# Two levels of seven products: where the inner seven stand among the outer ones, when their weights are split, and where one of their operands is kept

## The chip, the cores and the metric

The kernel runs on one core of a Trainium2 chip. The time is that of one execution on the device, in microseconds (us), and of several executions the median is taken. The engines of the core that matter here are TensorE (PE in the profile, with its weight loads shown apart as PEld), VectorE (DVE), ScalarE (ACT) and SyncE (SP), which issues nearly all transfers. Each engine works through its own list of instructions in a fixed order and waits at the head of that list until what the next instruction needs is there.

## The reference, cut to what matters

The program is a network of two layers over 1024 tokens of width 1024. Layer 0 mixes by attention, layer 1 by a gated recurrence, and behind each mixer stands the MLP that the change touches:

```python
def sqrelu_mlp(h, w_up, w_down):
    return jnp.square(jax.nn.relu(h @ w_up)) @ w_down

# in each of the two layers:
        h = rmsnorm(x, mlp_norm[layer])
        x = x + sqrelu_mlp(h, mlp_w_up[layer], mlp_w_down[layer]).astype(x.dtype)
```

Here `h` is 1024 by 1024 and `w_up` 1024 by 4096. The change is wholly in the product `h @ w_up`, called the up stage below; it comes once in each layer.

## The kernel before, in words

**A product in three.** All large products are made from float32 values that are split into a high part and a low part of the type that TensorE takes (`fp32r`). A split (`split`, `weight_split`, lines 458 and 469) is one copy that rounds, on ACT or DVE, and one subtraction on DVE. `mm3` (line 433) then issues three matmuls: high by high, high by low, low by high. A matmul has a 128x128 block of weights, and 512 columns of the other operand as a rule.

**The first level.** Each up stage works on 16 pairs of row blocks of the weights, `pair(m)` for m from 0 to 15 (line 757). A pair makes a 2 by 2 block of products by a Strassen scheme with seven products in place of eight. They are named 1 to 7 and stand in the order 1, 2, 5, 6, 3, 7, 4 (1, 5, 6, 2, 7, 3, 4 in the last pair). Each is 4 blocks times three matmuls of 512 columns, so twelve matmuls. Products 1, 6, 7 and 4 add up in one bank of PSUM (`main`), 5 and 3 in another (`side`), 2 in a third (`own`); between them the sums so far are copied out (`read`, `add_bank`). Behind the products stand the square of relu, the sums for the next Strassen scheme, and the stores of the results to DRAM (`kept`).

**The second level.** `INNER = (4,)` and `AT = 2` (lines 46 and 47): for the pairs from m = 4 on, product 4 of two neighbouring pairs, m and m + 1 with m even, is itself made by a Strassen scheme, in `inner` (line 693). So there are six groups of inner products in each layer, twelve in the kernel. Inner product k is two blocks times three matmuls of 256 columns, so six matmuls, and a group has 7 x 6 = 42. The inner products 1, 6, 7 and 4 add up in `main`, half of the first bank of the group; 5 and 3 in `side`, half of the second bank, and 2 in `own`, the other half of that second bank. After inner product 1, `take` (a copy on ACT or DVE) empties `main` before inner product 6 writes it, and so on. The order is fixed in lines 741 to 754: 1, take, 2, add, 6, take, 5, 7, take, add, 3, add, 4, take.

The weights of a group are four tiles: `a0`, `sa`, `sb`, and the far half of `a1`. They are split all together in lines 705 to 709, at the group's beginning. The other operands of inner products 5, 6, 7 and 4 are differences of quarters of `x[4]`; `prepare` (line 648) makes them once in each layer, during pair 2, splits them and stores the parts in DRAM, two transfers each. Each group loads them again, two tiles for each of these four inner products (lines 718 to 721). Inner products 1, 2 and 3 read halves of `x[4]` itself.

**What sets the order.** The code does not issue instructions as it runs. It first gives a list of operations to a planner (`Schedule`, line 146), which then places them on the engines by its own costs and latencies, always the ready operation of the lowest rank. The rank of a matmul is its place in the list (`now[i]`, line 205), counted in TensorE time; that of another operation is the time at which it is due. `lead = LEAD` brings it forward by 100 x 120 ns = 12 us. So what comes earlier in the list goes first on TensorE, as long as the planner believes it to be ready; otherwise TensorE gets the next one that is. The planner's beliefs that matter here: a matmul of 512 columns 216 ns; a slot of a ring of tiles usable 200 ns after its last reader; a copy of 512 columns 336 ns on DVE and 521 ns on ACT; a subtraction 603 ns; from DVE to TensorE 250 ns, from DVE to DVE 127 ns, from ACT to DVE 141 ns. Once placed, the order of each engine is fixed, and on the chip each engine waits for what is really there.

**Rings.** Tiles come from rings that are handed out in the order of the list: five slots for the high parts of weights (`wh`) and five for the low parts (`wl`), five for raw weights (`wr`), seven for sums of weights (`m`), twenty for other temporaries (`t`), four PSUM banks `p` (the banks of the inner groups and `own`) and four `q` (`main` and `side` of the pairs).

**Where the inner products stand.** In `pair`, the call `late = done[4]()` stands in the place of product 4 (lines 769 to 772). In the pair with even m this runs the whole of `inner`, so its seven products stand behind the six of the pair, one after another; the pair with m + 1 only takes the second half of the result.

Of the kernel before, what the change touches and what calls it, by code (L numbers as in the profile page):

```python
# [320 lines left out]
class Net:  # L321
# [326 lines left out]
    def prepare(self, name):  # L648

        near, far = slice(0, TH // 2), slice(TH // 2, TH)  # L650
        u = [self.t() for _ in range(HK)]
        for z, kept in zip(u, self.quarters[name]):
            self.dma(z, kept, 4 * P * TH)
        yield
        made = self.quarters[name] = {}

        def difference(out, x, y):
            for i in range(2):
                self.tt("any", out[:, i].only(i), x(i), y(i), ALU.subtract, TH // 2)

        def stored(k, t):
            made[k] = [self.keep(z.bitcast(F32)) for z in self.split(t.rearrange("p i c -> p (i c)"), self.t)]

        low, high = (lambda c: lambda i: u[i][:, c]), (lambda c: lambda i: u[2 + i][:, c])
        new = lambda: self.t(F32, (P, 2, TH // 2))
        part = lambda t: lambda i: t[:, i].only(i)
        t1 = new()
        difference(t1, low(far), low(near))
        stored(5, t1)
        yield  # L670
        t2 = new()
        difference(t2, high(far), part(t1))
        stored(6, t2)
        yield
        t3 = new()
        difference(t3, high(far), low(far))
        stored(7, t3)
        yield
        difference(t1, high(near), part(t2))
        stored(4, t1)  # L680
        yield

    def inner_of(self, name, m, x):
        got = []

        def of(i):
            if not got:
                got.extend(self.inner(name, m, x))
            return got[i]

        return of

    def inner(self, name, m, x):

        near, far, half = slice(0, TH // 2), slice(TH // 2, TH), TH // 2
        row, made = {2: 0, 4: 1}[name], self.quarters[name]
        self.s.lead = LEAD
        a0, a1 = (self.raw(self.io["up"][self.layer, i + row * (MT // 2)][:, TH:]) for i in (m, m + 1))
        sa, sb = self.t(tag="m"), self.t(tag="m")
        s1, s2, s3, s4 = sa[:, near].only(0), sa[:, far].only(1), sb[:, near].only(0), sb[:, far].only(1)  # L700
        self.tt("any", s1, a1[:, near], a1[:, far], ALU.add, half)
        self.tt("any", s2, s1, a0[:, near], ALU.subtract, half)
        self.tt("any", s3, a0[:, near], a1[:, near], ALU.subtract, half)
        self.tt("any", s4, a0[:, far], s2, ALU.subtract, half)
        wide = [self.weight_split(z) for z in (a0, sa, sb)]
        hi, lo = (self.tile(tag, BUFS[tag], (P, TH), F32R) for tag in ("wh", "wl"))
        self.copy(hi[:, far], a1[:, far], half, ("ACT", "DVE"), False)
        self.tt("any", lo[:, far], a1[:, far], hi[:, far].bitcast(F32), ALU.subtract, half)
        wide.append((hi, lo))
        w = {1: (0, near), 2: (0, far), 5: (1, near), 6: (1, far), 7: (2, near), 3: (2, far), 4: (3, far)}  # L710
        self.s.lead = 0
        banks = [self.psum(), self.psum()]
        main, side, own = banks[0][:, near].only(0), banks[1][:, near].only(0), banks[1][:, far].only(1)

        def product(k, ps, start):
            more = {} if start else {"skip_group_check": True}
            n, cols = w[k]
            if k in made:
                right = [self.t(F32R) for _ in range(2)]
                for z, kept in zip(right, made[k]):  # L720
                    self.dma(z.bitcast(F32), kept, 4 * P * TH)
            for i in range(2):
                c = slice(cols.start + i * P, cols.start + i * P + P)
                wh, wl = (z[:, c] for z in wide[n])
                if k in made:
                    xh, xl = (z[:, i * half : (i + 1) * half] for z in right)
                else:
                    at = near if k in (1, 2) else far
                    xh, xl = (z[:, at] for z in x[name][i if k == 1 else 2 + i])
                self.mm3(ps, (wh, wl), (xh, xl), start and i == 0, i == 1, half, slice(0, half), **more)  # L730

        y = [self.t(), self.t()]
        part = {(i, j): y[i][:, (near, far)[j]].only(j) for i in range(2) for j in range(2)}

        def take(z, bank):
            self.copy(halves(z), straight(bank), half)

        def add(z, bank):
            self.tt("DVE", halves(z), straight(bank), halves(z), ALU.add, half)

        product(1, main, True)
        take(part[0, 0], main)
        product(2, own, True)
        add(part[0, 0], own)
        product(6, main, False)
        take(part[0, 1], main)
        product(5, side, True)
        product(7, main, False)
        take(part[1, 1], main)
        add(part[1, 1], side)  # L750
        product(3, side, False)
        add(part[0, 1], side)
        product(4, main, False)
        take(part[1, 0], main)
        return y

    def pair(self, m, x, done, between=()):

        w = self.strassen_weights(*(self.io["up"][self.layer, i] for i in (m, m + MT // 2)), done)

        def read(ps):
            z = self.t()
            self.take(z, ps)
            return z

        main, side, own = self.psum("q"), self.psum("q"), None if 2 in done else self.psum()
        got = {}
        for name in (1, 5, 6, 2, 7, 3, 4) if m == MT // 2 - 1 else (1, 2, 5, 6, 3, 7, 4):
            if name in done:
                if name == 4:  # L770
                    late = done[4]()
                continue
            ps = main if name in (1, 6, 7, 4) else own if name == 2 else side
            self.product(ps, w[name], x[name], name in (1, 2, 5))
            if name == 1 and 2 in done:
                self.add_bank(done[2], main)
            elif name in (1, 5, 6, 7):
                got[name] = read(ps)
            for steps in between:
                next(steps, None)  # L780
        p5, u2, u3 = (got[name] for name in (5, 6, 7))

        def kept(name, z):
            self.hid[name, m] = self.keep(z)

        u1 = done[2] if 2 in done else got[1]
        if 2 not in done:
            self.add_bank(u1, own)
        h00 = self.square_relu(u1)
        kept(1, h00)  # L790
        self.add_bank(u2, side)
        h01, t5, t6, t4 = self.square_relu(u2), *(self.t() for _ in range(3))
        self.tt("any", t5, h01, h00, ALU.subtract)
        kept(5, t5)
        self.tt("any", p5, p5, u3, ALU.add)
        h11 = self.square_relu(p5)
        kept(3, h11)
        self.tt("any", t6, h11, t5, ALU.subtract)
        kept(6, t6)
        self.tt("any", h01, h11, h01, ALU.subtract)  # L800
        kept(7, h01)
        if 4 in done:
            self.tt("any", late, late, u3, ALU.add)
            h10 = self.square_relu(late)
        else:
            h10 = self.square_relu(main, True)
        kept(2, h10)
        self.tt("any", t4, h10, t6, ALU.subtract)
        kept(4, t4)

    def mlp(self, cut):

        x = self.mlp_second()
        steps = [self.prepare(name) for name in INNER]
        for m in range(0, MT // 2, 2):
            done = {}
            if m > AT:
                done = {name: self.inner_of(name, m, x) for name in INNER}
            for i in range(2):
                if m + i == MT // 2 - 2:  # L820
                    self.r = [self.a() for _ in range(NH)]
                    for hf in range(NH):
                        self.copy(self.r[hf], self.spread(self.square[hf]))
                if m + i == 1 and self.layer == 0:
                    self.hgrn_constants()
                self.pair(m + i, x, {name: y(i) if name == 2 else lambda y=y: y(i) for name, y in done.items()}, steps if m + i == AT else ())
        yield from self.down(cut)

    def hidden(self, name, p):
# [879 lines left out]
```

## Time and profile before

| what | value |
|---|---|
| median of 3 runs | 2011.96 us (2011.82 to 2012.09) |
| the profiled execution's own time | 2009.42 us |
| its span, first to last instruction | 2007.2 us |
| granted TensorE clock | 0.998 of full speed |
| VectorE busy | 1747.5 us (87%) |
| ScalarE busy | 1051.4 us (52%) |
| moved by DMA | 385.80 MB, 192 GB/s on average |

The up stage of layer 0 lies between about 325 and 605 us of the span, that of layer 1 between about 1420 and 1698 us. All instructions carry line 374, the line of the planner at which they are issued, so they are told apart by the tiles that they write and read: `q<-a,wh` with 512 columns are the outer products, `p<-a,wh` and `p<-t,wh` with 256 columns the inner products, where the operand read from `a` is `x[4]` and the one read from `t` has been loaded again from DRAM. `p<-a,wh` with 512 columns is product 2 of the pairs.

### The profile page before, as it was taken

The numbers are of one execution on the slowest core, as the hardware profiler recorded it, in microseconds if no ns is written. First come the engines' busy times: TensorE is split into PE (matmuls) and PEld (weight loads), VectorE is DVE, ScalarE is ACT, GpSimd is POOL, SyncE is SP. The second block draws the span as 40 slices with busy tenths as digits, with TensorE's granted clock in tenths as the row PEclk, the third lists the DMA queues.
The fourth block names the chain that finished last, engine by engine and source line by source line (L and its number), as shares of the span: only waits on it lengthen the run. The fifth ranks groups of instructions, "written<-read, shape, count | busy, mean of one in ns | idle before, by whom it ended". The sixth has DMA issues, their size and how long they took to land. (4 is left out here: it accounts for less than half of the span.)

```text
span 2007.2 us, 33753 instructions
## 1 busy us (share of the span) xinstructions
PE 1977.3 (99%) x11620; PEld 1720.8 (86%) x11620; DVE 1747.5 (87%) x3500; ACT 1051.4 (52%) x2141; POOL 62.2 (3%) x124
## 2 busy tenths in 40 slices
PE   9999999999999999999999999999999999999998
PEld 7877788888888888888888888888888888888887
DVE  8999899887788988799898999989987787897787
ACT  6567796555554423255345555554755556342353
POOL 4030100000000000000000000000000000000001
PEclk9999999999999999999999999999999999999999
DMA  6212364767678977745412212667577777897752
GB/s 217 89 53 63 122 225 156 275 216 231 231 228 287 312 262 259 237 163 175 146 62 80 76 59 90 206 205 255 179 248 231 231 226 246 290 324 230 234 180 84
DMA packets 218571, 385.80 MB, mean 192 GB/s; under 512 B 23968, under 2 KB 34208, under 8 KB 218400
## 3 DMA queue, kind: packets, MB, share of 16 engines
q1 hardware_dynamic: 217824, 383.13, 58.3%
q8 instruction: 91, 1.49, 0.3%
q14 instruction: 80, 0.66, 0.1%
q10 hardware_dynamic: 576, 0.52, 0.1%
HBM read 283.95 MB, written 99.61 MB: 191 GB/s over the span
## 5 line engine op out<-in xcount | busy, mean ns | idle before, releaser
L374 PE MATMUL q<-a,wh 128*128 128x512 f32 x2368 | 705.2, 379 | 1.8 <-DVE t L374 1.8
L374 PE MATMUL p<-a,wh 128*128 128x512 f32 (+1 forms) x2256 | 670.1, 376 | 0.8 <-DMA a<-d 0.6
L374 PEld LDWEIGHTS q<-a,wh 128*128 128x128 f32 x2368 | 445.6, 189 | 64.7 <-DVE t L374 2.6
L374 PEld LDWEIGHTS p<-a,wh 128*128 128x128 f32 x2256 | 417.3, 189 | 55.9 <-issue 1.2
L374 PE MATMUL q<-a,wl 128*128 128x512 f32 x1184 | 448.5, 379 | 0.0
L374 PE MATMUL p<-a,wl 128*128 128x512 f32 (+1 forms) x1128 | 421.4, 374 | 0.0
L374 ACT CAST a<-t 128x512 fp32r<-128x512 f32 x285 | 173.1, 619 | 272.6 <-PE q L374 138.9
L374 DVE TENSOR_TENSOR t<-t,t 128x512 f32<-128x512 f32 (+3 forms) x408 | 248.7, 633 | 22.2 <-ACT t L374 19.8
L374 ACT ACTIVATE t<-t 128x512 f32<-128x512 f32 x296 | 184.7, 630 | 140.4 <-DVE t L374 124.2
L374 PEld LDWEIGHTS q<-a,wl 128*128 128x128 f32 x1184 | 223.8, 189 | 31.3
L374 DVE TENSOR_TENSOR wl<-wr,wh 128x512 fp32r<-128x512 f32 x352 | 237.2, 676 | 11.6 <-ACT wh L374 4.1
L374 PEld LDWEIGHTS p<-a,wl 128*128 128x128 f32 x1128 | 213.6, 189 | 26.8 <-issue 0.4
L374 DVE TENSOR_TENSOR a<-t,a 128x512 fp32r<-128x512 f32 (+1 forms) x326 | 216.0, 682 | 4.5 <-ACT a L374 4.2
L374 DVE TENSOR_TENSOR wl<-m,wh 128x512 fp32r<-128x512 f32 x272 | 184.0, 684 | 7.5 <-ACT wh L374 1.9
L374 ACT CAST wh<-wr 128x512 fp32r<-128x512 f32 (+1 forms) x203 | 123.1, 609 | 121.8 <-PE p L374 45.2
L374 ACT COPY t<-q 128x512 f32<-128x512 f32 (+2 forms) x214 | 119.4, 560 | 88.4 <-PE q L374 86.9
L374 DVE TENSOR_TENSOR m<-wr,wr 128x512 f32<-128x512 f32 (+1 forms) x172 | 114.8, 669 | 39.5 <-DMA wr<-in_up 23.8
L374 ACT CAST wh<-m 128x512 fp32r<-128x512 f32 x166 | 101.4, 617 | 74.5 <-PE p L374 34.6
L374 PE MATMUL p<-wh,a 128*128 128x512 f32 x352 | 111.0, 385 | 0.0
L374 PEld LDWEIGHTS q<-t,t 128*64 128x64 f32 (+1 forms) x2160 | 95.1, 144 | 13.8 <-issue 6.2
L374 PE MATMUL q<-t,t 128*64 128x32 f32 (+2 forms) x2160 | 104.2, 229 | 1.6 <-DVE t L374 1.3
L374 DVE CAST wh<-wr 128x512 fp32r<-128x512 f32 x149 | 63.0, 423 | 46.1 <-PE q L374 22.1
(136 smaller groups left out, 2208.2 us busy)
## 6 DMA issues: line engine op xcount, KB each, us to landing
t<-d SPq DMA_DIRECT2D x368, 256.0 KB, 4.6
d<-t SPq DMA_DIRECT2D x300, 256.0 KB, 3.0
wr<-in_down SPq DMA_DIRECT2D x256, 256.0 KB, 4.1
wr<-in_up SPq DMA_DIRECT2D x152, 256.0 KB, 3.3
a<-d SPq DMA_DIRECT2D x60, 256.0 KB, 5.1
wr<-in_wqkv SPq DMA_DIRECT2D x48, 256.0 KB, 2.9
d<-a SPq DMA_DIRECT2D x48, 256.0 KB, 3.5
wr<-in_win SPq DMA_DIRECT2D x48, 256.0 KB, 2.9
```

The costliest lines, as they stand in the source:

```text
L374: fn(*[place(a) for a in args], **{k: place(v) for k, v in kw.items()})
```

## The change

The matmuls stay as they are, in number and size. What moves or is made another way:

1. `inner` becomes a generator that stops behind each of its products, and `pair` gets it in the list `between`: after each of its own products the even pair advances it by one. The list given to the planner then reads P1, I1, P2, I2, P5, I6, P6, I5, P3, I7, P7, I3, I4, where P are the products of the pair and I those of the group.
2. The weights of the group are split where the product stands that first uses them: `a0` ahead of I1, `sa` ahead of I6, `sb` ahead of I7, the far half of `a1` ahead of I4.
3. These splits, and the loads of the other operands, carry `lead = LEAD`; the loads did not before.
4. The operand of I5 is no longer split by `prepare` and stored in two parts, but stored once unsplit (so `prepare` also needs a fourth tile of its own, `t4`). A new generator, `put_in`, runs during pair 3: behind that pair's product 4 it loads the tile once and splits it into the far halves of `x[4][0]` and `x[4][1]`, which no inner product reads. I5 then reads it from there in each group, and the two loads for each group go away.
5. The result tiles `y` come into being inside the generator; `late = done[4]()` now only fetches them, and stands where the sum `late + u3` is made.

```diff
@@ prepare
         t1 = new()
         difference(t1, low(far), low(near))
-        stored(5, t1)
+        made[5] = self.keep(t1.rearrange("p i c -> p (i c)"))
         yield
...
-        difference(t1, high(near), part(t2))
-        stored(4, t1)
+        t4 = new()
+        difference(t4, high(near), part(t2))
+        stored(4, t4)
         yield
+
+    def put_in(self, name, x):
+
+        far, t1 = slice(TH // 2, TH), self.t()
+        for _ in range(6 if name == 4 else 1):
+            yield
+        self.dma(t1, self.quarters[name].pop(5), 4 * P * TH)
+        for i in range(2):
+            hi, lo, t = x[i][0][:, far].only(1), x[i][1][:, far].only(1), t1[:, i * (TH // 2) : (i + 1) * (TH // 2)]
+            self.copy(hi, t, TH // 2, ("ACT", "DVE"), False)
+            self.tt("any", lo, t, hi.bitcast(F32), ALU.subtract, TH // 2)
+        yield
@@ inner
-        wide = [self.weight_split(z) for z in (a0, sa, sb)]
-        hi, lo = (self.tile(tag, BUFS[tag], (P, TH), F32R) for tag in ("wh", "wl"))
-        self.copy(hi[:, far], a1[:, far], half, ("ACT", "DVE"), False)
-        self.tt("any", lo[:, far], a1[:, far], hi[:, far].bitcast(F32), ALU.subtract, half)
-        wide.append((hi, lo))
+        wide = []
         w = {1: (0, near), 2: (0, far), 5: (1, near), 6: (1, far), 7: (2, near), 3: (2, far), 4: (3, far)}
...
             n, cols = w[k]
+            self.s.lead = LEAD
+            if n == 3:
+                hi, lo = (self.tile(tag, BUFS[tag], (P, TH), F32R) for tag in ("wh", "wl"))
+                self.copy(hi[:, far], a1[:, far], half, ("ACT", "DVE"), False)
+                self.tt("any", lo[:, far], a1[:, far], hi[:, far].bitcast(F32), ALU.subtract, half)
+                wide.append((hi, lo))
+            elif n == len(wide):
+                wide.append(self.weight_split((a0, sa, sb)[n]))
             if k in made:
                 right = [self.t(F32R) for _ in range(2)]
                 for z, kept in zip(right, made[k]):
                     self.dma(z.bitcast(F32), kept, 4 * P * TH)
+            self.s.lead = 0
...
-                    xh, xl = (z[:, at] for z in x[name][i if k == 1 else 2 + i])
+                    xh, xl = (z[:, at] for z in x[name][i if k in (1, 5) else 2 + i])
...
-        y = [self.t(), self.t()]
+        y.extend(self.t() for _ in range(2))
...
         product(1, main, True)
         take(part[0, 0], main)
+        yield
         product(2, own, True)
         add(part[0, 0], own)
+        yield
         product(6, main, False)
         take(part[0, 1], main)
+        yield
         product(5, side, True)
+        yield
         product(7, main, False)
         take(part[1, 1], main)
         add(part[1, 1], side)
+        yield
         product(3, side, False)
         add(part[0, 1], side)
+        yield
         product(4, main, False)
         take(part[1, 0], main)
-        return y
+        yield
@@ pair
             if name in done:
-                if name == 4:
-                    late = done[4]()
                 continue
...
             for steps in between:
                 next(steps, None)
+        for steps in between:
+            run(steps)
...
         if 4 in done:
+            late = done[4]()
             self.tt("any", late, late, u3, ALU.add)
@@ mlp
+        made, n = {}, MT // 2
+        for m in range(n):
+            between, first = [], m - m % 2
+            if m == AT:
+                between += [self.prepare(name) for name in INNER]
+            if m == AT + 1:
+                between += [self.put_in(name, x[name]) for name in INNER]
+            for name in INNER:
+                c = first if name == 4 else first + 2
+                if AT < c < n and m % 2 == (name == 2):
+                    made[name, c] = []
+                    between.append(self.inner(name, c, x, made[name, c]))
...
+            self.pair(m, x, done, between)
```

More of the change, by code (lines that the diff above doesn't have):

```diff
@@ L678, in prepare, with inner @@
         yield
-        difference(t1, high(near), part(t2))
-        stored(4, t1)
+        t4 = new()
+        difference(t4, high(near), part(t2))
+        stored(4, t4)
         yield
[L683 to L693, printed above, removed]
+    def put_in(self, name, x):
[8 more added lines that the diff above has]
+        yield
+    def inner(self, name, m, x, y):
         near, far, half = slice(0, TH // 2), slice(TH // 2, TH), TH // 2
@@ L813, in mlp @@
         x = self.mlp_second()
[L814 to L826, printed above, removed]
+        made, n = {}, MT // 2
[10 more added lines that the diff above has]
+                    between.append(self.inner(name, c, x, made[name, c]))
+            done = {name: made[name, first][m % 2] if name == 2 else lambda: made[4, first][m % 2] for name in INNER if (name, first) in made}
+            if m == n - 2:
+                self.r = [self.a() for _ in range(NH)]
+                for hf in range(NH):
+                    self.copy(self.r[hf], self.spread(self.square[hf]))
+            if m == 1 and self.layer == 0:
+                self.hgrn_constants()
+            self.pair(m, x, done, between)
         yield from self.down(cut)
```

## The prediction

> **What bounds the kernel now.** I read the page first, for the share of each engine and of the clock.
>
> ```profile
> span 2007.2 us, 33753 instructions
> ## 1 busy us (share of the span) xinstructions
> PE 1977.3 (99%) x11620; PEld 1720.8 (86%) x11620; DVE 1747.5 (87%) x3500; ACT 1051.4 (52%) x2141; POOL 62.2 (3%) x124
> ...
> PEclk9999999999999999999999999999999999999999
> ```
>
> TensorE is busy 99% of the span at full clock, and the change takes no matmul away. So all that it can win is time in which TensorE stands still, and I have to find how much of that lies in the two up stages. Busy time is a poor measure of it, since the ends of matmuls are modelled. Starts are measured, so I go by pitch: the chain of waits for the outer products, the timeline of TensorE in the fourth group of layer 0 for the inner ones.
>
> ```profile
> 1703.79 2.59 PE p L374 x12
> ```
>
> ```profile
> 512.20 0.38 PE L374 MATMUL p<-a,wh 128*128 128x256 f32 x2
> 512.42 0.28 PE L374 MATMUL p<-a,wl 128*128 128x256 f32 x1
> 512.54 0.39 PE L374 MATMUL p<-a,wh 128*128 128x256 f32 x2
> ...
> 513.54 0.39 PE L374 MATMUL p<-t,wh 128*128 128x256 f32 x2
> 515.04 0.49 PE L374 MATMUL p<-t,wh 128*128 128x256 f32 x2 [1.12 <-ACT t L374]
> ```
>
> Twelve matmuls of 512 columns take 2.59 us, 216 ns each; twelve of 256 columns, the inner products 1 and 2, go from 512.20 to 513.54, 112 ns each. The last row is a real stop: two matmuls at 112 ns would have let the next start at 513.76, and it starts at 515.04, 1.28 us late. Next the table of windows over both up stages and over a stretch of pairs without inner products, and the rows of 256 columns from the groups by form.
>
> ```profile
> 325.00:605.00 280.00, 277.52 (x1404) 245.09 (x1403) 234.43 (x454) 156.83 (x285) 0.36 (x2) 1.00 0.69 230
> 1420.00:1698.00 278.00, 275.38 (x1394) 243.17 (x1393) 230.03 (x420) 156.71 (x284) 0.00 (x0) 1.00 0.71 232
> 335.00:400.00 65.00, 65.00 (x303) 56.76 (x302) 58.53 (x132) 39.87 (x71) 0.00 (x0) 1.00 0.79 271
> ```
>
> ```profile
> L374 PE MATMUL p<-t,wh 128*128 128x256 f32 x192 | 36.6, 281 | 4.6 <-ACT t L374 3.5 <-DVE t L374 1.0
> L374 PE MATMUL p<-t,wl 128*128 128x256 f32 x96 | 27.2, 284 | 0.5
> L374 PE MATMUL p<-a,wh 128*128 128x256 f32 x144 | 25.3, 275 | 0.0
> ```
>
> The third window, without inner products: 303 x 0.216 = 65.4 us of 65.0, nothing lost. In layer 0, 252 of the 1404 matmuls have 256 columns (six groups of 42) and 16 are short ones of about 0.11 us: 1136 x 0.216 + 252 x 0.112 + 1.8 = 275.4 of 280.0, so 4.6 us lost; in layer 1 1126 x 0.216 + 30.0 = 273.2 of 278.0, 4.8 lost. Together 9.4 us. The idle time shown before inner matmuls is only 4.6 + 0.5 = 5.1, since each stop hides the modelled tail of the matmul before it. A third count is the idle time of the weight loads, from the waits of PEld in the same two windows:
>
> ```profile
> PEld p L374 <- ACT t L374: 2.5, 4, 1.3
> PEld p L374 <- DVE t L374: 1.9, 6, 0.5
> ...
> PEld p L374 <- ACT t L374: 2.4, 3, 0.9
> PEld p L374 <- DVE t L374: 1.9, 6, 0.5
> ```
>
> 8.7 us in 19 stops, every one before a `p` bank, none for weights. I take **8.6 us** as what the inner groups cost in stops, 0.7 us for each of twelve.
>
> Why they stop, from the timeline of ACT and DVE beside the 1.28 us:
>
> ```profile
> 512.43 1.29 ACT L374 ACTIVATE t<-t 128x512 f32<-128x512 f32 x2 [2.43 <-DMA wr<-in_up]
> 513.63 0.60 ACT L374 CAST wh<-wr 128x512 fp32r<-128x512 f32 x1
> 514.14 0.58 ACT L374 COPY t<-q 128x512 f32<-128x512 f32 x1
> 514.62 0.38 ACT L374 COPY t<-p 128x256 f32<-128x256 f32 x1
> ```
>
> ```profile
> 509.18 0.69 DVE L374 TENSOR_TENSOR m<-wr,wr 128x512 f32<-128x512 f32 x1 [1.74 <-DMA wr<-in_up]
> ```
>
> I6 must not write `main` before `take` has read I1 out of it, and between them stands only I2, 6 x 0.112 = 0.67 us. The planner set I6 where it believed the `take` done; on the chip ACT was late, because DVE had waited 1.74 us for raw weights and the relu behind it came late. The `take` ran at 514.62, and everything on TensorE stood behind I6.
>
> **The change part by part.** *Weaving.* Between I1 and I6 now stand I2, P5 and perhaps P6, between I6 and I7 stand I5 and P3, between I7 and I3 stands P7. Each P is 12 x 0.216 = 2.59 us of cover where the longest stop was 1.28 on top of 0.67. So all 19 stops go: **-8.6 us**, bounds -9.4 and -5.1.
>
> One of the stops has another cause. In the second group:
>
> ```profile
> 441.67 0.42 DVE L374 TENSOR_TENSOR t<-p,t 128x256 f32<-128x256 f32 x1
> 441.80 0.71 PE L374 MATMUL p<-t,wl 128*128 128x256 f32 x2
> ```
>
> Two matmuls take 0.71 where they take 0.39 above: the second waits for the addition that still reads `own`. It writes `side`, which the planner books as a separate part of the same bank. The same stop returns if I5 follows I2 closely; here P5 and I6 lie between. The Trainium skill, "PSUM — Partial Sum Buffer", section "PSUM bank collisions raise a hardware error", says to guard a bank by bank and quadrant and not by address, since two engines in one bank collide even at disjoint columns. The 0.3 us of this row agree with it. By the planner's booking alone the stop would not exist, by the rule it comes back wherever I5 is set within an addition of I2; the sum is the same by both.
>
> *Weights one by one.* What is late next is the weights. The ring of five `wh` and `wl` is handed out in the order of the list, and that order stays: the pair's P1, P5, P2, P6, P3, P7, then `a0`, `sa`, `sb`, `a1`. So `a0` gets its slot, as now, when P2 is over. In the old order I1 came after four more products, some 10 us later. In the new list it comes *before* P2, so TensorE takes it the moment the planner believes the split done: no slack. The second such point is I6: `sa` gets the slot that `a0` leaves after I2. `sb` and `a1` have P3 and P7 between and keep more than 2.59 us. So there are two bare points for each group, 24 in all. The trace has this split with its times, in the first and in the slowest of the twelve groups:
>
> ```profile
> 392.18 0.38 PE L374 MATMUL p<-a,wl 128*128 128x512 f32 x1
> 392.38 0.43 DVE L374 CAST wh<-wr 128x512 fp32r<-128x512 f32 x1 [0.78 <-PE p L374]
> 393.32 0.68 DVE L374 TENSOR_TENSOR wl<-wr,wh 128x512 fp32r<-128x512 f32 x1
> ...
> 501.63 0.38 PE L374 MATMUL p<-a,wl 128*128 128x512 f32 x1
> 502.74 0.62 ACT L374 CAST wh<-wr 128x512 fp32r<-128x512 f32 x1
> 503.91 0.68 DVE L374 TENSOR_TENSOR wl<-wr,wh 128x512 fp32r<-128x512 f32 x1
> ```
>
> From the start of P2's last matmul to the end of the split: 1.82 and 2.96 us. The planner's own earliest belief, with its numbers: 0.216 + 0.200 + 0.336 + 0.127 + 0.603 + 0.250 = 1.73 with the copy on DVE, 1.93 on ACT. So the chip is 0.09 us late in the first and 1.03 in the slowest. A bare point cannot gain, so the bounds are 0 and 1.03 each, 0 and 24.7 us in all. In the first group DVE had been waiting 0.78 us for TensorE, that is, it was early; that is the usual case, so I price 23 points like it and one like the slowest: 23 x 0.09 + 1.03 = **+3.1 us**. Behind a point that waits stand the rest of P5 or P6 and all TensorE.
>
> The Trainium skill, "TensorE: Matmul & The Clock Gate", section "Step-by-step: what each phase is for", has it that only weight loads are pulled ahead and the matmuls themselves stay in program order. It speaks against this change: the ready matmuls of P5 cannot pass an I1 that waits. The trace agrees: behind the I6 that waited TensorE issued nothing for 1.28 us. If matmuls could pass one another the 3.1 us would be 0 and the time 2003.4; by the rule they stand.
>
> *Transfers and the kept operand.* Twelve groups lose two loads each, 24 of 256 KB; each layer loses one store and gains one load.
>
> ```profile
> t<-d SPq DMA_DIRECT2D x368, 256.0 KB, 4.6
> d<-t SPq DMA_DIRECT2D x300, 256.0 KB, 3.0
> ```
>
> They become 346 and 298. DMA is 0.69 and 0.71 busy in the two windows and TensorE never waits for a load there, so the gain is 0. The loads of I6, I7 and I4 get 12 us of lead and pass stores and raw weights on SP; their ring of 20 tiles has two users fewer for each group and holds one result tile for about a pair longer, so I cost it at 0. `put_in` is two copies and two subtractions of 256 columns, once in each layer, for one full split saved in `prepare`; it lies under P1 and P2 of pair 4 (5.2 us), since I1 cannot come before `a0`. Without that cover it would be at most the longer split above, 2.96 us for each layer. DVE, at 234.43 of 280.00 us, gets no more work.
>
> *Sum.* -8.6 + 3.1 = -5.5 us. The profiled execution took 2009.42 us, 2.2 more than its span; so 2003.9 for it, and against the median of 2011.96, **2006.5 us**.
>
> **The rivals.**
> *A new wait of the same size (B).* The bare points cost 0.2 to 0.5 us each, 4.6 to 12.6 in all, and the sum is nothing: 2008 to 2016. For it: the slowest split; against it: DVE was early in the first.
> *Slower (C).* The slowest split is the rule, because DVE and ACT run behind a late load of raw weights just there: this wait has its total in the waits of DVE.
>
> ```profile
> DVE m L374 <- DMA wr<-in_up: 24.7, 25, 1.7
> ```
>
> About 1.0 us each. At 24 points of 1.03 the change costs 24.7 - 8.6 = 16.1, so 2028; it is slower from 8.6 + 4.0 = 12.6 us on, 0.53 for each point. For it: the load at 509.18 is wanted 7.55 us after P2's end began, not far behind I6. Against it: `sa` should be split before that load lands.
> *The weave does not happen (D).* If the planner believes `a0` and `sa` so late that the inner products again stand together, the stops remain: 2012.
>
> **How the numbers follow.** 0.2% is 4.0 us, about what a measurement of this kernel can tell from no change. Forecast with the stops gone and small new waits (2002.6 to 2007.9): 0.58. B: 0.28, D: 0.06, both within 0.2%. C: 0.08. Range 2003.0 to 2012.5: below it lies only a nearly full 9.4, above it the worse half of B, and C.
>
> **What would show it.** Outer and inner rows in turn in the timeline, one inner product or two, then rows of `q`; 48 of the 192 `p<-t,wh` of 256 columns turn into `p<-a,wh`. PEld waits on `p` for ACT t and DVE t near 0 in both windows. New waits of `p` on ACT wh or DVE wl, some 3 us: over 8 is B, over 12 is C. The windows' lost time, by the same count, falls from 9.4 to about 4. The rest of the kernel keeps its stops; if the recurrence between 860 and 1330 us changes by over 2 us, my sum is wrong for a reason outside it.

## The result, and the profile after

The changed kernel takes 1998.07 us (median of four executions, 1995.56 to 2000.15), the kernel before beside it 2011.89 (2008.63 to 2012.09). The ratio is 0.9935, with an interval of 0.9917 to 0.9952: 13 us faster, where 5.5 was forecast. 1998.07 lies below the range that was given (2003.0 to 2012.5). The direction was right, the size too small by 8.4 us.

The profiled execution took 2000.15 us. First the page of the changed kernel: its span, the engines, and the two groups of transfers that the change touches.

```profile
span 1998.4 us, 33734 instructions
PE 1975.6 (99%) x11620; PEld 1724.4 (86%) x11620; DVE 1748.2 (87%) x3504; ACT 1046.6 (52%) x2141; POOL 60.7 (3%) x124
...
t<-d SPq DMA_DIRECT2D x346, 256.0 KB, 4.4
d<-t SPq DMA_DIRECT2D x298, 256.0 KB, 3.1
```

The counts are those of the working, 346 and 298. TensorE is "99% busy" before and after; the 13 us don't show in that number. They show in the table of windows, here over both up stages and over the recurrence (columns as before: length, then busy time and instructions of PE, PEld, DVE, ACT and POOL, clock, DMA share, GB/s).

```profile
325.00:602.00 277.00, 277.00 (x1414) 246.59 (x1413) 236.17 (x463) 153.33 (x284) 0.36 (x2) 1.00 0.66 218
1416.00:1690.00 274.00, 273.49 (x1394) 242.28 (x1393) 229.69 (x424) 152.19 (x281) 0.00 (x0) 1.00 0.68 224
860.00:1330.00 470.00, 467.11 (x3961) 409.43 (x3960) 428.40 (x936) 247.45 (x477) 8.14 (x18) 1.00 0.39 121
```

The count by pitch, as in the prediction: 268 of the matmuls in an up stage are the 252 of the inner products and 16 short ones, 30.0 us together; the others take 0.216 us each. Layer 0: (1414 - 268) x 0.216 + 30.0 = 277.5 of 277.0 us; layer 1: 1126 x 0.216 + 30.0 = 273.2 of 274.0. Nearly nothing is lost now, -0.5 + 0.8 = 0.2 us, where the same count in the first profile of before gave 9.4. In the recurrence PE is idle for 2.9 of 470 us; in the same window of before it was 3.7. What lies outside the up stages has not moved by over 2 us.

The groups by form, and the waits of PEld in the window 1420 to 1690 of the changed kernel:

```profile
L374 PE MATMUL p<-a,wh 128*128 128x256 f32 x192 | 33.8, 275 | 0.0
L374 PE MATMUL p<-t,wh 128*128 128x256 f32 x144 | 26.6, 275 | 0.0
```

```profile
PEld q L374 <- ACT t L374: 2.1, 5, 0.7
```

48 instructions have gone from `p<-t,wh` (192) to `p<-a,wh` (144 before), and nothing is idle ahead of any inner matmul. No wait on `p` is left; in the window of layer 0 PEld has no wait at all. The one row that is left is that of outer products.

That the weave happens, and how fine it is, shows in the timeline of the first group, TensorE and then DVE:

```profile
394.25 0.38 PE L374 MATMUL p<-a,wl 128*128 128x512 f32 x1
394.47 0.59 PE L374 MATMUL q<-a,wh 128*128 128x512 f32 x2
394.90 0.38 PE L374 MATMUL q<-a,wl 128*128 128x512 f32 x1
395.11 0.61 PE L374 MATMUL p<-a,wh 128*128 128x256 f32 x4
395.56 0.60 PE L374 MATMUL q<-a,wh 128*128 128x512 f32 x2
395.99 0.38 PE L374 MATMUL q<-a,wl 128*128 128x512 f32 x1
396.21 0.38 PE L374 MATMUL q<-a,wh 128*128 128x512 f32 x1
396.42 0.27 PE L374 MATMUL p<-a,wl 128*128 128x256 f32 x1
```

```profile
394.45 0.43 DVE L374 CAST wh<-wr 128x512 fp32r<-128x512 f32 x1
394.79 0.68 DVE L374 TENSOR_TENSOR t<-p,t 128x512 f32<-128x512 f32 x1
395.39 0.68 DVE L374 TENSOR_TENSOR wl<-wr,wh 128x512 fp32r<-128x512 f32 x1
```

The first row is P2's last matmul. The high part of `a0` is there at 394.45 + 0.43 = 394.88; the four matmuls of I1 that need only the high part start at 395.11, 0.23 us later. Then come outer matmuls, and the first of I1 that needs the low part (there at 395.39 + 0.68 = 396.07) starts at 396.42, 0.35 us later. The planner does not weave product by product but matmul by matmul. Measured the same way at all twelve groups, TensorE comes 0.23 to 0.26 us after the high part at I1, 0.20 to 0.35 after the low part, and 0.35 to 0.57 after the high part at I6. None of the 24 points called bare in the prediction waits.

So two things ask for an answer: why these points cost nothing, and where some 5 us more came from.

### The profile page after: what moved, and what is told of

Its sections match the earlier page's. It is cut to its first block, busy times and chain, and to the rows that moved or that the text cites. A ratio compares the mean times of both kernels' runs of the same rounds, so it can differ in the third digit from the quotient of the medians.

```text
span 1998.4 us, 33734 instructions
## 1 busy us (share of the span) xinstructions
PE 1975.6 (99%) x11620; PEld 1724.4 (86%) x11620; DVE 1748.2 (87%) x3504; ACT 1046.6 (52%) x2141; POOL 60.7 (3%) x124
## 5 line engine op out<-in xcount | busy, mean ns | idle before, releaser
L374 PE MATMUL p<-a,wh 128*128 128x512 f32 (+1 forms) x2304 | 679.1, 375 | 0.2
L374 PEld LDWEIGHTS p<-a,wh 128*128 128x128 f32 x2304 | 425.9, 190 | 56.2 <-issue 1.2
L374 PE MATMUL p<-a,wl 128*128 128x512 f32 (+1 forms) x1152 | 426.6, 372 | 0.0
L374 ACT CAST a<-t 128x512 fp32r<-128x512 f32 x295 | 178.8, 619 | 271.4 <-PE q L374 136.0
L374 PEld LDWEIGHTS p<-a,wl 128*128 128x128 f32 x1152 | 217.6, 190 | 26.9 <-issue 0.4
L374 ACT CAST wh<-m 128x512 fp32r<-128x512 f32 x153 | 93.0, 616 | 57.4 <-PE q L374 36.6
L374 DVE CAST wh<-m 128x512 fp32r<-128x512 f32 x119 | 50.6, 425 | 58.3 <-PE q L374 35.7
```

What stands on the lines that cost most here:

```text
L374: fn(*[place(a) for a in args], **{k: place(v) for k, v in kw.items()})
```

## The experiments

The prediction's steps belong to parts of the change that can be made singly: point 1 (weave), 2 (splits one by one), 3 (lead of the loads), 4 (operand kept). All were timed in five rounds beside the kernel before on the same chip. For each the table gives the median, that of the kernel before beside it, the ratio with its interval, the lost time of both up stages in its profile by the count above (windows 325 to 602 and 1416 to 1690), and DVE's total wait for raw weights.

| kernel | us | before | ratio | lost, us | DVE wait, us |
|---|---|---|---|---|---|
| before, second profile | 2012.85 | 2011.33 | 1.0008 [0.9999, 1.0017] | 14.9 | 31.7 |
| lead alone (3) | 2007.31 | 2012.33 | 0.9976 [0.9966, 0.9986] | 5.6 | 15.4 |
| operand alone (4) | 2006.49 | 2012.62 | 0.9969 [0.9957, 0.9981] | 5.4 | 22.5 |
| weave alone (1) | 2003.74 | 2012.62 | 0.9958 [0.9945, 0.9972] | 6.9 | 28.9 |
| weave and operand (1, 4) | 2002.98 | 2010.58 | 0.9959 [0.9945, 0.9974] | 4.1 | 20.6 |
| all but the lead (1, 2, 4) | 2004.40 | 2011.33 | 0.9965 [0.9951, 0.9978] | 5.9 | 22.7 |
| the same, raw weights earlier | 2005.03 | 2012.33 | 0.9961 [0.9949, 0.9974] | 5.4 | 21.7 |
| all but the weave (2, 3, 4) | 2004.89 | 2012.62 | 0.9962 [0.9950, 0.9975] | 5.4 | 11.9 |
| woven by twos | 2000.33 | 2011.33 | 0.9949 [0.9936, 0.9961] | 2.0 | 7.9 |
| weave and lead (1, 3) | 2000.40 | 2012.33 | 0.9938 [0.9924, 0.9952] | 1.5 | 15.7 |
| all but the operand (1, 2, 3) | 1999.45 | 2010.58 | 0.9940 [0.9922, 0.9959] | 0.2 | 14.5 |
| all but the splits (1, 3, 4) | 1997.25 | 2011.33 | 0.9933 [0.9920, 0.9945] | 0.5 | 15.7 |
| change, unread loads added | 1999.06 | 2010.58 | 0.9938 [0.9921, 0.9955] | 0.2 | 17.8 |
| change, bytes alone added | 1999.61 | 2010.58 | 0.9939 [0.9922, 0.9956] | 1.8 | 17.6 |
| change, collisions added | 2002.64 | 2009.81 | 0.9962 [0.9949, 0.9976] | 3.1 | 40.2 |
| change, again | 1998.08 | 2012.62 | 0.9931 [0.9917, 0.9945] | 0.5 | 17.3 |
| change, once more | 1998.04 | 2009.81 | 0.9937 [0.9925, 0.9950] | 0.5 | 13.2 |

**The change again.**

> The changed kernel itself, once more, with more executions. Theory 1 (the gain is the stops before the p banks and nothing else): the stops were worth 8.6 to 9.4 us, and the two first profiles differ by 9.3, so a ratio of 0.9953 to 0.9957, 8.6 to 9.4 us below before; the 13.8 us between the first medians is then spread between executions. Theory 2 (something beside the stops gains 4 to 5 us more): 12 to 14 us below before again, ratio 0.9930 to 0.9940.

> The changed kernel beside it on the same chip: 0.992 to 0.9945 of before, DVE waits for wr<-in_up 16 to 19 us, no wait for ACT wh or DVE wl.

The changed kernel itself, timed beside the others: 0.9931 and 0.9937. The gain is there each time.

**The weave alone.** The splits stand together at the group's head again, the loads have no lead, and I5's operand is loaded for each group:

```diff
...
-        wide = []
+        wide = [self.weight_split(z) for z in (a0, sa, sb)]
...
-            self.s.lead = LEAD
...
-                    xh, xl = (z[:, at] for z in x[name][i if k in (1, 5) else 2 + i])
+                    xh, xl = (z[:, at] for z in x[name][i if k == 1 else 2 + i])
```

> Only point 1 of the change: the inner products woven between the pair's, their weights split together at the head of the group, I5 loaded for each group, loads without lead. Theory 1: all of the gain, within 1 us of the changed kernel in the same call; waits of PEld on p for ACT t and DVE t near 0. Theory 2 (fewer transfers and the kept operand bring part): 3 to 5 us slower than the changed kernel.

8.9 us faster than before, but 5.7 slower than the change beside it. Its waits of PEld in the windows 325 to 605 and 1420 to 1690:

```profile
PEld p L374 <- DVE wl L374: 1.7, 4, 0.5
PEld p L374 <- ACT wh L374: 1.4, 3, 0.7
...
PEld p L374 <- ACT wh L374: 4.4, 4, 2.0
PEld p L374 <- DVE wl L374: 2.0, 4, 0.5
```

The old releasers (ACT `t`, DVE `t`) are gone; new ones stand there, the copies and subtractions of weights. All of them stand at I1, one of the two points of each group that the prediction called bare. They are 9.5 us by this view; by the starts of the matmuls the first of I1 that needs the low part comes 6.7 us late, over all twelve groups. At I6, the other such point, no matmul starts late, here or in any other woven kernel. The longest wait, in the ninth group, in the timelines of DVE, ACT and TensorE (the bracket is the idle time before an instruction and what ended it):

```profile
1548.94 0.69 DVE L374 TENSOR_TENSOR m<-wr,wr 128x512 f32<-128x512 f32 x1 [2.69 <-DMA wr<-in_up]
```

```profile
1551.47 2.48 ACT L374 ACTIVATE t<-t 128x512 f32<-128x512 f32 x4 [3.15 <-DVE t L374]
1553.86 0.57 ACT L374 COPY t<-q 128x512 f32<-128x512 f32 x1
1554.32 0.62 ACT L374 CAST wh<-wr 128x512 fp32r<-128x512 f32 x1
```

```profile
1552.20 0.38 PE L374 MATMUL p<-a,wl 128*128 128x512 f32 x1
...
1553.06 0.38 PE L374 MATMUL q<-a,wh 128*128 128x512 f32 x1
1555.00 0.71 PE L374 MATMUL p<-a,wh 128*128 128x256 f32 x4 [1.56 <-ACT wh L374]
```

Raw weights land late, DVE stands for 2.69 us, its late results leave ACT idle for 3.15 and then with four relus in a row, and the copy of `a0` comes behind them at 1554.32. P2's last matmul started at 1552.20. I1 starts at 1555.00, where 1553.06 + 0.22 = 1553.28 was possible: 1.72 us lost. This is rival C's chain to the letter. It decides only at some of the points, and in the change at none.

**Everything but the weave.**

```diff
             for steps in between:
-                next(steps, None)
+                if steps.gi_code.co_name != "inner":
+                    next(steps, None)
```

> Points 2 to 5 without point 1: the seven inner products stand together behind the pair's six as before, but weights are split one by one, loads have lead, and the operand of I5 is kept. Theory 1: as before, within 2 us of it, with PEld waits on p of 7 to 10 us in the two up stages. Theory 2: 3 to 5 us faster than before.

2004.89: the weave is worth 6.8 us on top of the rest. The stops before `p` return, but with 4.3 us in eight waits of PEld, not 8.7 in 19: the lead and the operand kept shorten them even in the old order.

**The operand alone**, in the old order:

> Point 4 alone: the operand of I5 kept in the idle halves of x[4], 22 loads and 2 stores fewer; order, splits and lead as before. Theory 1: within 2 us of before, stops as before. Theory 2 (transfers): 3 to 5 us faster than before.

6.1 us faster, which the prediction held to be 0. Yet it vanishes beside the others. Weave and operand without the rest (its edit is the weave alone plus point 4):

> The changed kernel without points 2 and 3: woven, operand of I5 kept, but the group's weights split together at its head and loads without lead. Theory A: within 1.5 us of the changed kernel, ratio 0.992 to 0.994, bare points without waits. Theory B: 4 to 6 us slower, bare points waiting for ACT wh and DVE wl as in the weave alone.

0.9959, as the weave alone. And everything but the operand:

> The changed kernel without point 4: woven, weights split one by one, loads with lead, but the operand of I5 split by prepare, stored in two parts and loaded for each group. Theory A (the kept operand, by taking transfers out of the stage, is worth 4 to 6 us beside the weave): 4 to 6 us slower than the changed kernel, like the weave alone (ratio 0.9955 to 0.9965), with PEld waits on p for ACT wh and DVE wl of 3 us or more. Theory B (splitting one by one and the lead are what cures the bare points): within 1.5 us of the changed kernel, those waits near 0.

0.9940 against 0.9931 and 0.9937 of the change: no difference that the intervals show. Two more kernels give the change back the transfers that point 4 took, as loads that nobody reads, once into the ring `t` and once (208 KB each in place of 256) into a tile of their own, so without a use of the ring:

```diff
             if k in made:
+                if k == 5:
+                    for kept in made[6]:
+                        self.dma(self.t(), kept, 4 * P * TH)
```

```diff
+                if k == 5:
+                    for kept in made[6]:
+                        self.dma(self.idle, kept[:, :416], 4 * P * TH)
```

> The changed kernel, with two loads of 256 KB for each group put back at I5 into two tiles of the ring t, which nothing reads: the transfers and the ring slots of the old way, with the operand still taken from x[4]. Theory A: 4 to 6 us slower than the changed kernel, as if I5 loaded its operand. Theory C (what counts in point 4 is not the loads but where the I5 matmuls read, or prepare): within 1.5 us of the changed kernel.

> The changed kernel, with two loads of 208 KB for each group put back at I5 into a tile of its own that nothing reads: the bytes and the places on SP's queue, but no slot of the ring t. Theory A1 (the traffic itself and SP's queue): 3 to 6 us slower than the changed kernel. Theory A2 (the slots of the ring t): within 1.5 us of the changed kernel, while loads_back is slower.

0.9938 and 0.9939: neither the 24 loads nor their slots of the ring are worth anything measurable in the woven kernel with lead. There the 0 of the prediction holds.

**Splits or lead.** Two kernels, each the change without one of them: the splits stand together as in the weave alone, with the lead kept; or the lead ends ahead of the loads:

```diff
             elif n == len(wide):
                 wide.append(self.weight_split((a0, sa, sb)[n]))
+            self.s.lead = 0
             if k in made:
```

> The changed kernel without point 2: woven, operand kept, loads with lead, but the group's weights split together at its head. Theory B1 (splitting one by one is what spares the bare points): 4 to 6 us slower than the changed kernel, ratio 0.995 to 0.997, with waits of inner matmuls for ACT wh and DVE wl of 3 us or more. Theory B2 (the lead of the loads): within 1.5 us of the changed kernel, those waits near 0.

> The changed kernel without point 3: woven, operand kept, weights split one by one, but loads without lead. Theory B1: within 1.5 us of the changed kernel, ratio 0.992 to 0.995, waits for ACT wh and DVE wl near 0. Theory B2: 4 to 6 us slower, with those waits.

This is the pair that decides. Without the splits one by one: 1997.25, as fast as the change. Without the lead: 2004.40, so 7.2 us between the two, and the waits on `p` are back. The two kernels differ in point 2 as well, which has no worth that shows; against the change itself the ratios give 5.6 to 6.8 us for the lead (0.9965 against 0.9931 to 0.9937). PEld in the windows 325 to 605 and 1420 to 1690 of the kernel without lead:

```profile
PEld p L374 <- DVE wl L374: 2.0, 4, 0.5
PEld p L374 <- ACT wh L374: 1.5, 3, 0.6
...
PEld p L374 <- DVE wl L374: 1.8, 4, 0.5
...
PEld p L374 <- ACT wh L374: 1.6, 2, 0.9
PEld p L374 <- DVE wh L374: 0.6, 1, 0.6
```

Two further kernels turn this round: only weave and lead, and only the lead in the kernel before.

```diff
             if k in made:
+                self.s.lead = LEAD
                 right = [self.t(F32R) for _ in range(2)]
                 for z, kept in zip(right, made[k]):
                     self.dma(z.bitcast(F32), kept, 4 * P * TH)
+                self.s.lead = 0
```

> Points 1 and 3 alone: woven, loads with lead; weights split together at the head of the group, operand of I5 loaded for each group as before. Theory E (the weave and the lead are the whole change): within 2 us of the changed kernel, ratio 0.992 to 0.995, waits of inner matmuls for ACT wh and DVE wl under 1 us. Rival (points 2 or 4 are needed too): 4 us or more slower than the changed kernel, like the weave alone at 0.9958.

> Point 3 alone in the kernel before: the loads for the inner products get lead, nothing else. Theory E1 (the lead matters only for the bare points that the weave makes): within 2 us of before, 0.999 to 1.001, the stops for ACT t and DVE t stay. Theory E2 (the lead by itself lets raw weights and with them DVE and ACT run on time): 4 to 6 us faster than before, 0.997 to 0.998, with shorter stops.

Weave and lead alone give 0.9938, the whole change as far as can be measured. The lead alone, a change of two lines that touches only loads for which TensorE never waited, gives 0.9976, some 5 us.

**How the lead acts.** Two theories. F: unled loads go out on SP beside the raw weights of the next pair and make them late, and the chain shown above follows. G: the lead makes the planner place other work otherwise, and with it I1. For F stands the last column of the table: with lead DVE waits 7.9 to 17.8 us for raw weights (18.6 in the first profile of the change; the kernel with collisions is left aside), without it 20.6 to 31.7. The first attempt to tell them apart left the loads without lead and gave the raw weights of the pair and the group another 12 us:

```diff
+        self.ahead = 2 * LEAD
         w = self.strassen_weights(*(self.io["up"][self.layer, i] for i in (m, m + MT // 2)), done)
+        self.ahead = LEAD
```

> The changed kernel without point 3 (loads without lead), but with the raw weights of the up stage brought forward by another 12 us. Theory F (without lead the bare points wait because raw weights land late on DVE, and ACT's copy of a0 behind it): the raw weights no longer late, DVE waits for wr<-in_up well under 18 us in all, waits for ACT wh and DVE wl near 0, within 2 us of the changed kernel. Rival G (the planner places DVE's and ACT's work about the bare points another way, whatever the raw weights do): 4 to 6 us slower than the changed kernel, waits for ACT wh and DVE wl as in the run without lead.

It told nothing: the raw weights did not land earlier (DVE waits 21.7 us, without the edit 22.7). Their slots in the ring of five, not their rank, set when they go out: in the window 325 to 605 SP stands for 59.2 us before loads because of the instructions on DVE that read the raw tiles out (`m` 38.0, `wl` 21.2), without the edit for 59.6. The second attempt put the collisions into the change: six loads for each group that nobody reads, without lead, due with I6, I7 and I4.

```diff
             self.s.lead = 0
+            late = [self.t() for _ in range(2)] if k in (6, 7, 4) else []
+            for z in late:
+                self.dma(z, self.quarters[4][6][0], 4 * P * TH)
```

> The changed kernel, with its own loads led as they are, and six more loads of 256 KB for each group that nothing reads, without lead, due for I6, I7 and I4 as the real ones are without lead (the planner books them as wanted by these products, the chip waits for none). Theory F (loads without lead go out beside the raw weights that DVE waits for, and make them late): more t<-d issues within 2.5 us of such raw loads, near the 1.1 to 1.6 of the runs without lead against 0 to 0.8 with it; DVE waits for wr<-in_up over 20 us; waits for ACT wh and DVE wl back; 3 us or more slower than the changed kernel. Rival G (it is the planner's placing and not the loads): within 2 us of the changed kernel, those waits near 0.

2002.64 beside 1998.04 for the change: 4.6 us slower. The waits of DVE for raw weights, of the change once more and of this kernel (total, times, longest):

```profile
DVE m L374 <- DMA wr<-in_up: 13.2, 23, 1.2
```

```profile
DVE m L374 <- DMA wr<-in_up: 40.2, 30, 3.7
```

Loads at these due times do make the raw weights late, and that costs time: F has a part. How large it is in the change can't be read from this, since 72 loads are added here, where the lead only moves those that are there; the 24 unread loads of the two kernels above went out with lead, and cost nothing that shows. But the small stops that recur in each layer without lead, `p` on DVE `wl` four times with 1.8 to 2.0 us, did not come back as such: here there are two of 0.7 us in all in layer 0 and one of 1.8 in layer 1. They have another ground, in the order. I counted the matmuls between P2's last and the first of I1 that needs the low part, at 0.216 and 0.112 us each. With lead, with or without the collisions, the second starts 2.18 us behind the first in four groups and 2.39 in eight; without lead 2.18 in the same four and 1.96 or less in the other eight. The low part is there after 1.82 to 2.19 us in the change. So in eight groups the order without lead asks for it too early, which makes eight stops, 3.8 us of waits. G has a part too. The split itself also ends later without lead: in those eight groups the low part is there 2.07 to 2.97 us behind P2's last matmul, in the change 2.11 to 2.19. The first matmul of I1 that needs it comes 4.8 us late without lead, over all groups; had it the order of the change and its own late splits, some 2.4 us of that would be left, by an estimate from these starts. So order and late splits have about equal parts at I1.

**Woven by twos**: the group advances two products at once, behind P2, P6 and P7 only.

```diff
-                next(steps, None)
+                if steps.gi_code.co_name != "inner":
+                    next(steps, None)
+                elif name in (2, 6, 7):
+                    next(steps, None)
+                    next(steps, None)
```

> The changed kernel with the inner products woven in by twos: I1 and I2 behind P2, I6 and I5 behind P6, I7 and I3 behind P7, I4 at the end. I3 and I4 again follow I7 with little between, so the copy and the addition that empty the bank lose their cover, I6 and I7 keep it. Cover theory: 0.2 to 0.5 us of stop for each group at I3 or I4, 2 to 6 us in all, so 2 to 6 us slower than the changed kernel. Rival (any weaving will do): within 1.5 us of it.

2000.33 against 1997.25 beside it for the change without point 2: 3 us dearer, in the expected span. Only part of its stops are of the kind that was expected before I3 and I4. Of the 3.9 us that PEld waits on `p` there, 1.3 are for an addition (DVE `t`); the rest is for split weights. So the cover of a whole P between neighbours is worth 3 us at most, and most of the gain is had with less.

**The kernel before, profiled again.**

> The kernel before, unchanged, for a second profiled execution. The first profile of before lost 9.4 us in the up stages and its time, 2009.4, lies 2.6 below its median. Theory S (the stops are longer in ordinary executions than in that profile): this profile, if its time is nearer 2012, loses 2 to 3 us more in the up stages, at the same places. Theory N (the difference lies elsewhere in the program): the up stages lose 9 to 10 us again. Ratio 0.999 to 1.001.

This execution took 2014.57 us, the first profiled one 2009.42. Its waits of PEld in the windows 325 to 605 and 1420 to 1700:

```profile
PEld p L374 <- ACT t L374: 5.8, 3, 2.7
PEld p L374 <- DVE t L374: 1.7, 5, 0.5
...
PEld p L374 <- ACT t L374: 2.8, 3, 1.1
PEld p L374 <- DVE t L374: 1.9, 6, 0.5
```

The rows on DVE `t`, the additions into the same bank, are as they were, 3.6 us beside 3.8. Those on ACT `t`, the `take` behind late raw weights, have grown from 4.9 to 8.6 us. Together 12.2 us where the prediction read 8.7. By pitch the lost time is 14.9 us, not 9.3 in the same windows, and the difference of 5.6 is about that of the two executions, 5.15. Some 1.7 us of the 14.9 are no stop but a stretch at half clock, shown at the end. Subtract the lost time of each of the 19 profiles from its execution's own time, and 1995.3 to 2003.7 is left, 1998.8 on average; what is left does not follow which points of the change a kernel has, though it scatters by 8 us. By that estimate the kernel before, with medians of 2009.8 to 2012.9, usually loses 11 to 14 us in its up stages. The first profile was a mild one.

## Why the prediction was right in direction and wrong in size

- **What bounds the kernel: right.** TensorE's standing still in the inner groups was all that there was to win, and the change wins it: lost time 0.2 to 0.5 us in three profiles. Everything else stayed.
- **The removed stops: mechanism right, size too small.** "So all 19 stops go: -8.6 us" took its number from one execution, and so did its bounds. That execution was 2.5 us quicker than the median, and the prediction said so, but it subtracted its stops from the median all the same. The stops on ACT `t` were longer in the execution in which DVE waited longer for raw weights (8.6 us with 31.7, 4.9 with 24.7), and the lost time by pitch was 14.9 and 9.3 us. By the estimate above about 13 go in the typical one, so 4 to 5 us of the error lie here; with the 3.1 of the next step that is nearly all of the 8.4.
- **The bare points: the step that failed.** "23 x 0.09 + 1.03 = +3.1 us" measured 0. That I1 has no slack by the list's order is right: weave alone shows it waiting, 6.7 us by starts, and all but the lead shows it again. That I6 has none is wrong, for it waits in no woven kernel; what gives it its slack was not followed up. In the change the slack is 0.20 to 0.57 us at every point. The row taken for the usual case, 1.82 us from P2's last matmul to the end of the split, holds in four of the twelve groups, in the profile of before as in that of the change. In the other eight, where ACT makes the copy, the same count gives 2.06 to 2.96 us before the change and 2.11 to 2.19 in it, so by its own rows the working priced these too low. They cost nothing because TensorE asks later than the working took from the planner's numbers. In the four groups it first takes four matmuls that need no low part, then outer ones, and asks for the low part 2.17 us behind P2's last (394.25 to 396.42), not after 1.73. In the eight it asks after 2.39, not after 1.93; without the lead it asks after 1.96 there, nearly as in the working, and the waits are real.
- **The lead of the loads: the step that failed with it.** "I cost it at 0" rested on the ring of 20 tiles; that these loads "pass stores and raw weights on SP" was said and not priced. Alone it brings 5 us, within the woven kernel 6 to 7. The profile held a sign of it in a row that the prediction quoted, DVE's wait for raw weights of 24.7 us; it was used for rival C only, and it was not asked which transfers make these raw weights late. So the lead is also the reason why rival C stayed away: without it the chain is real, and all but the lead still comes out at 0.9965, for the new waits eat part of the gain but not all.
- **Splits one by one and the operand kept: 0, as forecast,** in the woven kernel with lead. That the operand alone brings 6 us in the old order was not foreseen. Effects on the same stops don't add: 5 (lead), 6 (operand) and 9 (weave) alone, 13 together.
- **The rule on program order** (the Trainium skill, "TensorE: Matmul & The Clock Gate", section "Step-by-step: what each phase is for") is borne out by the 1.56 us at 1555.00, behind which outer matmuls stood. It didn't decide the time, since the planner had set outer matmuls ahead of the point.

What stays open: how the 6 to 7 us of the lead divide between late raw weights and the planner's placing outside I1, and why the lead changes that placing. The kernel with collisions has the change's order at I1 and loses 4.6 us, but its raw weights are later (40.2 us of waiting) than those of the kernel without lead (22.7). And by what the operand alone wins 6 us: the stops behind `take` are nearly gone there (PEld waits 1.1 us on `p` for ACT `t`, where it was 4.9), but DVE waits about as long for raw weights (22.5) as in the kernel before (24.7).

## What to carry to other kernels

A load that nobody waits for can still be worth microseconds: before a moved or led transfer is priced at nothing, look which just-in-time loads share its queue at its old and its new place, and what hangs on those. Stops read from one profile are a sample: where the profiled execution lies off the median, the stops it shows are off too, and a second profile costs little. Small dependent products woven among long independent ones lose their stops, and the next thing to look at is the operand that now has to be ready first.

## What the hardware showed besides

In three of the 19 profiles a stretch at half rate follows a stop of TensorE in mid-execution. In the first profile of the change, at the beginning of layer 0's up stage, from the timeline of TensorE and the table of windows:

```profile
317.97 1.05 PE L374 MATMUL q<-c,t 128*128 128x1 f32 x8 [1.07 <-DVE t L374]
...
320.31 1.06 PE L374 MATMUL q<-a,wh 128*128 128x512 f32 x2
321.17 0.64 PE L374 MATMUL q<-a,wl 128*128 128x512 f32 x1
321.59 1.06 PE L374 MATMUL q<-a,wh 128*128 128x512 f32 x2
322.45 0.64 PE L374 MATMUL q<-a,wl 128*128 128x512 f32 x1
```

```profile
316.80:320.20 3.40, 2.33 (x15) 2.10 (x15) 3.40 (x6) 2.51 (x5) 0.00 (x0) 1.00 0.11 40
320.20:323.60 3.40, 3.40 (x10) 2.69 (x9) 3.40 (x7) 2.28 (x4) 0.00 (x0) 0.50 0.46 133
```

From 320.31 to 322.45 five matmuls of 512 columns take 2.14 us, 428 ns each in place of 216, and the granted clock was 0.50 from 320.20 to 323.60. The next profile of the same kernel has 216 at the same place, behind a stop of 0.75 us. The stretch cost about 1.7 us of that execution, half of its 3.4. But the first profile of the kernel before has full clock behind a stop of 1.20 us at this place, so the length of the one stop doesn't decide. In the second profile of the kernel before such a stretch stands from 443.5 to 447 us, behind its longest stop:

```profile
442.82 0.49 PE L374 MATMUL p<-t,wh 128*128 128x256 f32 x2 [2.51 <-ACT t L374]
...
443.48 0.92 PE L374 MATMUL p<-t,wl 128*128 128x256 f32 x2
```

The third profile is that of the kernel woven by twos, with a granted clock of 0.50 from 1060.80 to 1064.20, behind a stop of 0.82 us. So a stop can cost more than its own length; when it does, these runs don't show. The Trainium skill, "TensorE: Matmul & The Clock Gate", section "What's actually happening", gives half of the clock as the idle state, after an idle window of about 3.4 us. The halving agrees with the 428 ns and the granted 0.50; the single stops ahead of it were 1.07, 2.51 and 0.82 us, shorter than that window.
